# Order of the first loads, square buffers, and the places of u, the chunk inputs and po in a weight-streaming trunk

## The chip, the cores and the metric

The kernel runs on one core of one Trainium2 chip. The metric is the device time of one execution in microseconds. Three runs of the kernel before gave 935.23, 936.41 and 936.98 us, a median of 936.41 us.

The engines are TensorE (PE in the profile; PEld is its weight load), VectorE (DVE), ScalarE (ACT), GpSimd (POOL) and SyncE (SP). Here SyncE issues nearly all transfers.

## The reference

Two layers with D = 2048 and 256 positions. In each, one projection of the normalised input feeds two groups of heads: differential attention and a diagonal state space (S5).

```
for l in range(2):
    h = rmsnorm(x, pre_norm_g[l])
    q, k, v, z_att, u, z_ssm = split(h @ w_in[l])          # 6 x 1024 columns
    w = softmax(q1 k1 + bias) - lam * softmax(q2 k2 + bias)  # 8 heads, chunk-causal mask
    o_att = rmsnorm(w @ v) * (1 - lam_init) * silu(z_att)
    y = s5_ssm(u)             # 64 groups of 16 channels, 64 complex states each, scan over positions
    g_val, g_gate = split(gelu(y) @ w_glu[l])
    o_ssm = g_val * sigmoid(g_gate) * silu(z_ssm)
    x = x + rmsnorm(concat(o_att, o_ssm) @ w_out[l])
```

## The kernel before

**Streaming.** All weights of both layers lie in one tensor of 144 chunks, taken in 288 half-steps of 512 KB (`raw`, 128 x 1024 float32), 144 to a layer. `emit_dma` (line 197) issues the load of a half-step on SyncE's queue into one of five buffers, in order; a load waits on the queue until its buffer is free, and what is written behind it on that queue waits too. Each half-step is split for TensorE: ScalarE copies it to `hi` (rounded, line 158), VectorE subtracts to get `lo` (line 140). Then `main` issues the half-step's matmuls into a PSUM bank `ac` of a pool of four banks: weights hi with both pieces of h (`ht`), and lo with the first. In layer 0 the half-steps of u, q and k have 24 matmuls, in layer 1 (`JOIN`) 16, most others 12.

**Order in a layer.** Half-steps 0 to 7 give the first four blocks of u by another split of the work (four `ac` banks, all held until u is evacuated), 8 to 15 the remaining u chunks 4 to 7, 16 to 47 q and k, then v and the gates, the GLU and the output projection. The index of a half-step within its layer is `s`.

**What runs beside it.** Everything else is written as Python generators that are woven into the half-steps: each half-step advances every live generator to its next `yield` (ahead of its lo), and after its matmuls those that stand at `yield 1` or `yield 2`, up to a fixed allowance. So one further `yield` puts what follows it one half-step later in the order of every engine. Short VectorE operations that generators append to `urgent` or `weave` are filled in around the lo of a half-step.

- `rstd_gen` computes the pre-norm. In layer 0: squares of x on ScalarE and sums on VectorE (`sq`), `psv` on TensorE, Newton steps on VectorE, `psr` on TensorE, `rbc` on ScalarE. Only then can VectorE make `u` from the held banks, which also frees them. Two of the u chunks (4 and 5) accumulate in banks of the other PSUM pool (`acu`).
- `u_store` and `u_load` (lines 678 and 687) write u to DRAM and read it back in another layout (`U`), in two halves, called from `hooks` at fixed `s`.
- `s_gen` makes the chunk inputs: it copies into H behind the matmuls `pss` of U with `wi`, in four parts of two blocks; the scan follows on VectorE. The third and fourth part wait for `u2`, which says that the second half of U is there.
- `pv_gen`, one per head: transposes the attention weights, copies them to `wt` (ScalarE), multiplies with v (`po`), squares and gates; every fourth head starts the Newton steps of the head norm (`scal`).

**The start.** `load_x` and `load_w0` bring the first two 128-column slices of x (on ScalarE's queue) and the first weight in two halves (on SyncE's); `build0(k)` makes h's two pieces of slice k, of which half-step 0 needs the first for its first half and the second for its second. Half-step 1 needs the next weight. W0 is a number of warm-up matmuls ahead of it.

Of the kernel before, what the change touches and what calls it, by code (L numbers as in the profile page):

```python
# [14 lines left out]
ALU = mybir.AluOpType  # L15
# [10 lines left out]
MAGIC = 12582912.0  # L26
SC = 57
Y0 = (80, 77)
W0 = 18
PS = 4  # L30
TB = 38
PG = 1
# [10 lines left out]
LB = 2  # L43
SX = 144
NA = 2
JOIN = (1,)
TPS = ([(0, 1024), (1024, 1024)], [(0, 512), (512, 768), (1280, 768)])
WY = 2
# [36 lines left out]
def hybrid_trunk(ctx: ExitStack, tc, x, rel_bias, post_norm_g, xt_in, wst, vecs, poles, lams, bc, onehot, out):  # L85
# [16 lines left out]
    def R(i, name, dt=F32):  # L102
        return rp.tile([128, 2048], dt, tag=f"r{i}", name=name)

    def side(name):
        return pb.tile([128, 512], F32, tag="side", name=name)

    def acc(name):
        return pa.tile([128, 512], F32, tag="acc", name=name)
# [29 lines left out]
    def tt(o, a, b, op):  # L139
        V.tensor_tensor(o, a, b, op=op)  # L140
        return cost(o)
# [15 lines left out]
    def act(o, i, f, **kw):  # L157
        A.activation(out=o, in_=i, func=f, **kw)  # L158
# [153 lines left out]
    def until(key):  # L312
        while key not in S:
            yield
# [310 lines left out]
    def rstd_gen(l):  # L625
        if l == 0:

            X = S["xT"].rearrange("p k c -> p (k c)")
            sq = R(1, "sq")
            a, b = sq[:, 0:1024], sq[:, 1024:2048]  # L630
            act(a, X[:, 0:1024], AF.Square)
            yield
            for n in range(1, 4):
                act(b, X[:, 1024 * n:1024 * n + 1024], AF.Square)
                yield
                tt(a, a, b, ALU.add)
            for n in (512, 256):
                tt(a[:, 0:n], a[:, 0:n], a[:, n:2 * n], ALU.add)
            yield 1
            psv = side("psv")  # L640
            for t in range(2):
                mm4(psv[:, 2 * t:2 * t + 2], a[:, 128 * t:128 * t + 128], ones[:, 0:2], True, True)
        else:
            xt = S["xt"]
            for n in range(4):
                for t in range(2):
                    j = tmp5("junk")
                    act(j, xt[t][:, 512 * n:512 * n + 512], AF.Square, accum_out=ssx[:, t, n:n + 1])
                yield
        dg = tmp("dg")  # L650

        def ops():
            v = st.tile([128, 2], F32, tag="nv", name="nv")
            if l == 0:
                ts(v, psv[:, 0:4:2], EPS * D, None, ALU.add)
            else:
                V.tensor_reduce(out=v, in_=ssx, axis=AX.X, op=ALU.add)
            yield 70
            yield from newton_ops(rst[:, 0], v, 2)
            yield ts(rst[:, 1], rst[:, 0], -0.5 * NK * DK, None, ALU.mult)  # L660
            yield ts(rst[:, 0], rst[:, 0], -NK * DK, None, ALU.mult)
            for t in range(2):
                yield ts(dg[:, 128 * t:128 * t + 128], ident, rst[:, 0, t:t + 1], None, ALU.mult)
            S[f"rst{l}"] = True

        urgent.append(ops())
        yield from until(f"rst{l}")
        yield 1
        ps = side("psr")
        mm4(ps[:, 0:256], ones, dg, True, True)  # L670
        act(rbc, ps[:, 0:256], AF.Copy)
        S[f"rbc{l}"] = True
        yield


    def u_store(b0):
        cut = lambda t: t.rearrange("p (m b c) -> p m (b c)", m=4, b=8)[:, :, 64 * b0:64 * b0 + 256]
        SY.dma_start(out=cut(uds), in_=cut(S["u"]))
# [34 lines left out]

    def s_gen(l):
        yield from until(f"wa{l}")
        H = rp.tile([128, 2, NPAIR, 64], F32, tag="big", name="H")
        S["H"] = H
        G.memset(H[:, :, :, 0:1], 0.0)
        U = S["U"]
        for b0 in range(0, 8, 2):  # L720
            while b0 >= 4 and not (S["u2"] and f"wi{l}" in S):
                yield
            yield 2

            pss = [side("pss") for _ in range(2)]
            for b in (b0, b0 + 1):
                wi = S[f"wi{l}" if b >= 4 else f"wa{l}"][b // 4]
                for h in range(2):
                    for a in range(2):
                        for r, g in ((0, 0), (1, 1), (1, 0), (0, 1)):  # L730
                            rows, o = slice(64 * g, 64 * g + 64), 64 * (g ^ r)
                            q, c = 2 * h + r, 256 * a + 64 * (2 * (b - b0) + h)
                            mm4(pss[r][o:o + 64, c:c + 64], wi[rows, b % 4, 2 * q + a], U[rows, 8 * q + b], True, True)
            yield
            for r, ps in enumerate(pss):
                psv = ps.rearrange("p (a j c) -> p a j c", a=2, j=4)
                hv = H[:, :, 4 * b0 + r:4 * b0 + 8:2]
                act(hv[:, :, :, 16:64], psv[:, :, :, 0:48], AF.Copy)
                act(hv[:, :, :, 1:16], psv[:, :, :, 48:63], AF.Copy)
        weave.append(scan_ops(l))  # L740
        yield

        src = uds.rearrange("(q g n) (m r) -> g m n q r", q=4, g=2, m=4)
        dst = U.rearrange("p (q b) c -> p q (b c)", q=4)
        for d in range(2):
            for m in range(4):
                r = 64 * d + 16 * m
                SY.dma_start(out=dst[r:r + 16, 1::2], in_=src[1 - d, m, :, 1::2])
            yield
# [130 lines left out]
    def pv_gen(l, h):  # L880
        yield from until(f"w{l}{h}")
        v, za, s1 = S["v"], S["za"], S["as"]
        w_ = S["att"][:, 384 * (h % 4):384 * (h % 4) + 384]
        yield 1
        ps = side("pwt")
        for j in range(3):
            tpose(ps[:, 128 * j:128 * j + 128], w_[:, 128 * j:128 * j + 128], ident)
        yield
        wt = scp.tile([128, 384], F32, tag="wt", name="wt")
        act(wt, ps[:, 0:384], AF.Copy)  # L890
        yield 1
        po = side("po")
        vv = v.rearrange("p (t c) -> p t c", t=2)[:, :, 128 * h:128 * h + 128]
        mm4(po[:, 0:128], wt[:, 256:384], vv[:, 0], True, True)
        mm4(po[:, 128:256], wt[:, 0:128], vv[:, 0], True, False)
        mm4(po[:, 128:256], wt[:, 128:256], vv[:, 1], False, True)
        yield
        for b in range(2):
            j = tmp("junk")
            act(j[:, 0:128], po[:, 128 * b:128 * b + 128], AF.Square, accum_out=s1[:, 2, 2 * h + b:2 * h + b + 1])  # L900
        zv = za.rearrange("p (t c) -> p t c", t=2)[:, :, 128 * h:128 * h + 128]
        mul(zv, zv, po[:, 0:256].rearrange("p (t c) -> p t c", t=2))
        S[f"att{l}{h}"] = True
        if h % 4 == 3:
            w = slice(2 * (h - 3), 2 * (h - 3) + 8)
            sc = st.tile([128, 8], F32, tag=f"scal{h // 4}", name="scal")
            lam_init = 0.8 - 0.6 * math.exp(-0.3 * l)

            def ops():
                a = st.tile([128, 8], F32, tag="a8", name="a8")  # L910
                yield mul(a, s1[:, 2, w], s1[:, 0, w])
                yield stt(a, a, 1.0 / 128, s1[:, 0, w], ALU.mult, ALU.mult)
                yield ts(a, a, EPS, None, ALU.add)
                yield from newton_ops(sc, a, 8)
                yield stt(sc, sc, -NK * (1.0 - lam_init), s1[:, 0, w], ALU.mult, ALU.mult)
                yield mul(sc.rearrange("p (h t) -> p h t", t=2), sc.rearrange("p (h t) -> p h t", t=2),
                          rst[:, 1].unsqueeze(1).to_broadcast([128, 4, 2]))
                S[f"scal{l}{h // 4}"] = sc

            yield  # L920
            urgent.append(ops())
# [87 lines left out]
    def main(hs, only=None, part=None):  # L1009
# [29 lines left out]
            done = b == 3 and h == 1  # L1039
        elif seg in ("u", "q", "k"):  # L1040
            if h == 0:
                S["acc"] = [side("acu") if i % LAYER in (4, 5) else acc("ac")]
            o = S["acc"][0][:, 0:256]
            hv = hi.rearrange("p (k c) -> p k c", k=8)
            lv = lo.rearrange("p (k c) -> p k c", k=8)
# [72 lines left out]
    def hooks(l, s):  # L1118
# [27 lines left out]
                SY.dma_start(out=S["xt"][t], in_=src[128 * t:128 * t + 128])  # L1146
        if s == 11:
            S["U"] = rp.tile([128, NPAIR, 64], F32, tag="U", name="U")
        if s in (14, 19):
            u_store(0 if s == 14 else 4)  # L1150
        if s in (15, 20):
            u_load(0 if s == 15 else 4)
        if s == 15:
            at(cur[0], s_gen(l))
        if s == 21:
            at(cur[0], toep_gen(l))
        S["u2"] = s >= 22
        S["zfree"] = s >= 113
        S["wfree"] = l > 0
        for h in range(8):  # L1160
# [19 lines left out]
    with tc.manual_schedule():  # L1180
# [9 lines left out]
        def load_w0(p):  # L1190
            c = slice(512 * p, 512 * p + 512)
            SY.dma_start(out=raw[0][:, c], in_=wst[0][:, c])


        load_params()
        raw[0] = wp.tile([128, 1024], F32, tag="raw", name="raw")
        load_w0(0)
        load_x(A, 0, 1)
        load_x(A, 1, 2)
        load_w0(1)  # L1200
        act(cf[:, 0, 0:2], ones[:, 0:2], AF.Tanh)
        emit_dma(1)
# [162 lines left out]
```

## Time and profile before

| | |
|---|---|
| median of three runs | 936.41 us |
| profiled execution | 934.74 us |
| its span | 933.0 us |
| TensorE busy | 905.2 us (97%) |
| VectorE busy | 672.1 us (72%) |
| ScalarE busy | 486.4 us (52%) |
| mean granted clock of TensorE | 0.987 |
| mean rate of the transfers | 189 GB/s |

The span runs from the first to the last instruction that the profiler recorded; the time is a little longer. Busy times count instructions that work, not those that wait. The granted clock is a share of TensorE's full speed: 1.0 is 2.4 GHz, 0.5 is 1.2 GHz. In a timeline row the bracket gives the idle time of that engine ahead of the row and what ended it.

### The profile page before, as it was taken

To read this page: it belongs to the slowest core of one execution; us is meant where nothing else is said; L and a number is where in the kernel's file an instruction comes from. 1 tells how busy PE (TensorE), PEld (TensorE's weight loads), DVE (VectorE), ACT (ScalarE), POOL (GpSimd) and SP (SyncE) were. 2 spreads that over 40 slices of the span, in tenths; PEclk is the share of its full clock that TensorE was granted. 3 is DMA by queue.
4 is the path that set the end of the run, shared out by engine and by line. 5 is a ranking of instruction groups with operands and counts; after the bars stand their busy time and mean duration, and the time that the engine had idled before them with its cause. 6 is when DMAs were issued, how large, how long until landed. Compare 5 with 4: busy or idle time off the path is not lost.

```text
span 933.0 us, 16359 instructions
## 1 busy us (share of the span) xinstructions
PE 905.2 (97%) x6354; PEld 778.5 (83%) x6354; DVE 672.1 (72%) x1202; ACT 486.4 (52%) x878; POOL 13.7 (1%) x19
## 2 busy tenths in 40 slices
PE   8999999999999999999999899999999999999995
PEld 8889999878778788888889688888888788888884
DVE  5878995898974757898576448899876466665464
ACT  5533348375365776444469344445565565644451
POOL 2000000000000000000000000000000000000001
PEclk9999999999999999999999999999999999999998
DMA  8657574775453477576645655865545346665752
GB/s 310 198 172 252 183 213 141 186 236 164 153 181 114 118 244 230 177 248 226 213 161 182 213 173 144 262 195 173 172 141 176 112 156 189 197 211 171 289 185 91
DMA packets 65069, 176.11 MB, mean 189 GB/s; under 512 B 17574, under 2 KB 24512, under 8 KB 64096
## 3 DMA queue, kind: packets, MB, share of 16 engines
q1 hardware_dynamic: 64416, 174.63, 59.1%
q8 instruction: 50, 0.82, 0.4%
q10 hardware_dynamic: 432, 0.29, 0.1%
q14 instruction: 27, 0.22, 0.1%
q0 software_dynamic: 144, 0.15, 0.0%
HBM read 167.42 MB, written 7.88 MB: 188 GB/s over the span
## 4 chain that ended last, share of the span: by engine, by line
PE 87%; DVE 6%; ACT 2%; DMA 2%; issue 1%; SPq 0%; ACTq 0%; DVEq 0%
PE ac L137 77%; PE acu L137 3%; DVE lo L140 2%; PE lga L137 1%; PE po L137 1%; PE psy L137 1%; DMA xT<-in_xt_dram 1%; PE pss L137 1%; DVE H L140 1%; PE psw L121 1%; ACT hi L158 1%; DVE sct L140 1%; DMA uds<-u 1%; DVE sq L140 1%; ACT y L158 0%
## 5 line engine op out<-in xcount | busy, mean ns | idle before, releaser
L158 ACT ACTIVATE hi<-raw 128x1024 fp32r<-128x1024 f32 (+1 forms) x282 | 297.7, 1057 | 360.6 <-PE ac L137 303.4
L140 DVE TENSOR_TENSOR lo<-raw,hi 128x1024 fp32r<-128x1024 f32 (+1 forms) x282 | 342.7, 1218 | 128.1 <-ACT hi L158 126.5
L137 PE MATMUL ac<-ht,hi 128*128 128x256 f32 (+1 forms) x1120 | 259.5, 318 | 4.3 <-DVE u L140 2.1
L137 PE MATMUL ac<-hi,ht 128*128 128x512 f32 x768 | 249.3, 396 | 0.0
L137 PEld LDWEIGHTS ac<-ht,hi 128*128 128x128 f32 x1120 | 187.4, 194 | 19.1 <-ACT hi L158 4.5
L137 PE MATMUL ac<-ht,lo 128*128 128x256 f32 x704 | 200.7, 286 | 0.6 <-DVE lo L140 0.6
L137 PEld LDWEIGHTS ac<-hi,ht 128*128 128x128 f32 x768 | 144.2, 188 | 31.5
L137 PE MATMUL ac<-lo,ht 128*128 128x512 f32 x384 | 150.3, 391 | 1.5 <-DVE lo L140 1.4
L137 PE MATMUL ac<-hi,mx 128*128 128x512 f32 x456 | 141.9, 390 | 0.0
L137 PEld LDWEIGHTS ac<-ht,lo 128*128 128x128 f32 x704 | 136.3, 194 | 1.1 <-DVE lo L140 1.1
L137 PEld LDWEIGHTS ac<-hi,mx 128*128 128x128 f32 x456 | 85.6, 188 | 17.9
L137 PE MATMUL ac<-lo,mx 128*128 128x512 f32 x228 | 88.7, 389 | 0.0
L137 PEld LDWEIGHTS ac<-lo,ht 128*128 128x128 f32 x384 | 72.2, 188 | 17.5 <-DVE lo L140 3.7
L137 PE MATMUL ac<-hi,ghi 128*128 128x512 f32 x128 | 51.6, 403 | 0.0
L137 PE MATMUL ac<-hi,glo 128*128 128x512 f32 x128 | 50.2, 392 | 0.0
L137 PEld LDWEIGHTS ac<-lo,mx 128*128 128x128 f32 x228 | 42.8, 188 | 8.7
L137 PE MATMUL ac<-lo,ghi 128*128 128x512 f32 x128 | 49.9, 390 | 0.0
L158 ACT ACTIVATE att<-att,mx 128x128 f32<-128x128 f32 x64 | 28.4, 446 | 4.8 <-DVE mx L863 4.2
L147 DVE SCALAR_TENSOR_TENSOR y<-y 128x512 f32<-128x512 f32 x16 | 11.0, 690 | 26.9 <-ACT y L158 26.9
L137 PEld LDWEIGHTS ac<-hi,glo 128*128 128x128 f32 x128 | 24.0, 188 | 5.3
L137 PEld LDWEIGHTS ac<-lo,ghi 128*128 128x128 f32 x128 | 24.1, 188 | 4.5
L137 PEld LDWEIGHTS ac<-hi,ghi 128*128 128x128 f32 x128 | 24.1, 188 | 4.5
(202 smaller groups left out, 963.4 us busy)
## 6 DMA issues: line engine op xcount, KB each, us to landing
raw<-in_wst_dram SPq DMA_DIRECT2D x287, 512.0 KB, 3.8
U<-uds SPq DMA_DIRECT2D x48, 64.0 KB, 2.5
bt<-in_bc_dram SPq DMA_DIRECT2D x4, 512.0 KB, 6.2
uds<-u SPq DMA_DIRECT2D x4, 512.0 KB, 5.0
pg<-in_post_norm_g_dram SPq DMA_DIRECT2D x2, 1024.0 KB, 6.9
xt<-in_x_dram SPq DMA_DIRECT2D x2, 1024.0 KB, 7.2
xt<-xsave SPq DMA_DIRECT2D x2, 1024.0 KB, 6.4
tabs<-tab SPq DMA_DIRECT2D x1, 1536.0 KB, 9.1
```

The lines of the kernel that those rows point to most:

```text
L121: P.transpose(o, i, idn)
L137: P.matmul(o, lhsT=l, rhs=r, start=start, stop=stop, skip_group_check=True)
L140: V.tensor_tensor(o, a, b, op=op)
L147: V.scalar_tensor_tensor(out=o, in0=a, scalar=s, in1=b, op0=op0, op1=op1)
L158: A.activation(out=o, in_=i, func=f, **kw)
```

## The change

- The two first slices of x move from ScalarE's queue to SyncE's, in the order slice 0, half weight 0, slice 1, half weight 1. W0 goes from 18 to 13.
- The four squares get a buffer each, in two more tiles. One `yield` more stands ahead of `psv`, and in layer 0 one more ahead of `psr`.
- In layer 0 the u chunks 4, 5 and 6 accumulate in the other pool, in layer 1 only chunk 4 (before, 4 and 5 in both).
- `u_store` comes at s = 15 and 20 in layer 0 and at 11 and 18 in layer 1 (before, 14 and 19 in both), the loads one half-step behind it.
- `s_gen` starts one half-step later and has another `yield` ahead of its third part.
- In `pv_gen`, `wt` comes from a pool with two buffers (before, one), and `po` one half-step later.

Order on SyncE at the start, before: the row that is not a weight is the later slices of x, the first two slices being on ScalarE's queue.

```order
L1192 DMA raw<-in_wst_dram 128x512 x2
L197 DMA raw<-in_wst_dram 128x1024
L1188 DMA xT<-in_xt_dram 128x512
L197 DMA raw<-in_wst_dram 128x1024
L1188 DMA xT<-in_xt_dram 128x512
```

The same place after:

```order
L1197 DMA xT<-in_xt_dram 128x256
L1201 DMA raw<-in_wst_dram 128x512
L1197 DMA xT<-in_xt_dram 128x256
L1201 DMA raw<-in_wst_dram 128x512
L199 DMA raw<-in_wst_dram 128x1024
L1197 DMA xT<-in_xt_dram 128x512
```

The slices of 256 columns stand between the two halves of weight 0 and ahead of the next weight now.

Order on VectorE behind `psr` of layer 0, before; u is made from the acu banks, then from the four held banks ac0 to ac3, and the lo of the coming half-step follows:

```order
L140 TENSOR_TENSOR u_503<-acu_601,rbc_100 128x16x4x4
L140 TENSOR_TENSOR u_503<-acu_521,rbc_100 128x16x4x4
L140 TENSOR_TENSOR u_503<-ac0_175,rbc_100 128x16x4x4
L140 TENSOR_TENSOR u_503<-ac1_176,rbc_100 128x16x4x4
L140 TENSOR_TENSOR u_503<-ac2_177,rbc_100 128x16x4x4
L140 TENSOR_TENSOR u_503<-ac3_178,rbc_100 128x16x4x4
L140 TENSOR_TENSOR lo_674<-raw_501,hi_666 128x1024
```

After:

```order
L142 TENSOR_TENSOR u_495<-acu_671,rbc_100 128x16x4x4
L142 TENSOR_TENSOR u_495<-acu_594,rbc_100 128x16x4x4
L142 TENSOR_TENSOR u_495<-acu_504,rbc_100 128x16x4x4
L142 TENSOR_TENSOR u_495<-ac0_170,rbc_100 128x16x4x4
L142 TENSOR_TENSOR u_495<-ac1_171,rbc_100 128x16x4x4
L142 TENSOR_TENSOR u_495<-ac2_172,rbc_100 128x16x4x4
L142 TENSOR_TENSOR u_495<-ac3_173,rbc_100 128x16x4x4
L142 TENSOR_TENSOR lo_748<-raw_576,hi_739 128x1024
```

One product more stands ahead of ac0. On TensorE `psr` stands, after the change, two half-steps further on, between the last matmul into acu_671 and the first into ac_750, which takes the bank of ac0:

```order
L139 MATMUL acu_671<-ht_159,hi_622 128x256 x2
L139 MATMUL acu_671<-ht_159,lo_626 128x256
L139 MATMUL psr_734<-dg_532,ones_91 128x256
L139 MATMUL ac_750<-ht_159,hi_661 128x256 x2
L139 MATMUL ac_750<-ht_159,lo_663 128x256
```

Before, it stood in the same way between acu_601 and ac_676.

Order on SyncE around the store and loads of u in layer 1, before:

```order
L197 DMA raw<-in_wst_dram 128x1024 x11
L678 DMA uds<-u 512x1x256
L197 DMA raw<-in_wst_dram 128x1024
L687 DMA U<-uds 16x4x256 x8
L197 DMA raw<-in_wst_dram 128x1024 x4
L678 DMA uds<-u 512x1x256
L197 DMA raw<-in_wst_dram 128x1024
L687 DMA U<-uds 16x4x256 x8
```

After:

```order
L199 DMA raw<-in_wst_dram 128x1024 x8
L683 DMA uds<-u 512x1x256
L199 DMA raw<-in_wst_dram 128x1024
L692 DMA U<-uds 16x4x256 x8
L199 DMA raw<-in_wst_dram 128x1024 x6
L683 DMA uds<-u 512x1x256
L199 DMA raw<-in_wst_dram 128x1024
L692 DMA U<-uds 16x4x256 x8
```

The first store has moved ahead of three weight loads, the second ahead of one.

```diff
@@ -26,7 +26,7 @@
 MAGIC = 12582912.0
 SC = 57
 Y0 = (80, 77)
-W0 = 18
+W0 = 13
 PS = 4
 TB = 38
 PG = 1
@@ -43,6 +43,8 @@
 LB = 2
 SX = 144
 NA = 2
+ACU = ((4, 5, 6), (4,))
+US = ((15, 20), (11, 18))
 JOIN = (1,)
 TPS = ([(0, 1024), (1024, 1024)], [(0, 512), (512, 768), (1280, 768)])
 WY = 2
@@ -626,16 +628,17 @@
         if l == 0:
 
             X = S["xT"].rearrange("p k c -> p (k c)")
-            sq = R(1, "sq")
-            a, b = sq[:, 0:1024], sq[:, 1024:2048]
+            sq = [t[:, 1024 * i:1024 * i + 1024] for t in (R(1, "sq"), R(0, "sq")) for i in range(2)]
+            a = sq[0]
             act(a, X[:, 0:1024], AF.Square)
             yield
             for n in range(1, 4):
-                act(b, X[:, 1024 * n:1024 * n + 1024], AF.Square)
+                act(sq[n], X[:, 1024 * n:1024 * n + 1024], AF.Square)
                 yield
-                tt(a, a, b, ALU.add)
+                tt(a, a, sq[n], ALU.add)
             for n in (512, 256):
                 tt(a[:, 0:n], a[:, 0:n], a[:, n:2 * n], ALU.add)
+            yield
             yield 1
             psv = side("psv")
             for t in range(2):
@@ -665,6 +668,8 @@
 
         urgent.append(ops())
         yield from until(f"rst{l}")
+        if l == 0:
+            yield
         yield 1
         ps = side("psr")
         mm4(ps[:, 0:256], ones, dg, True, True)
@@ -713,12 +718,15 @@
 
     def s_gen(l):
         yield from until(f"wa{l}")
+        yield
         H = rp.tile([128, 2, NPAIR, 64], F32, tag="big", name="H")
         S["H"] = H
         G.memset(H[:, :, :, 0:1], 0.0)
         U = S["U"]
         for b0 in range(0, 8, 2):
-            while b0 >= 4 and not (S["u2"] and f"wi{l}" in S):
+            if b0 == 4:
+                while not (S["u2"] and f"wi{l}" in S):
+                    yield
                 yield
             yield 2
 
@@ -886,8 +894,9 @@
         for j in range(3):
             tpose(ps[:, 128 * j:128 * j + 128], w_[:, 128 * j:128 * j + 128], ident)
         yield
-        wt = scp.tile([128, 384], F32, tag="wt", name="wt")
+        wt = st.tile([128, 384], F32, tag="wt", name="wt")
         act(wt, ps[:, 0:384], AF.Copy)
+        yield
         yield 1
         po = side("po")
         vv = v.rearrange("p (t c) -> p t c", t=2)[:, :, 128 * h:128 * h + 128]
@@ -1039,7 +1048,7 @@
             done = b == 3 and h == 1
         elif seg in ("u", "q", "k"):
             if h == 0:
-                S["acc"] = [side("acu") if i % LAYER in (4, 5) else acc("ac")]
+                S["acc"] = [side("acu") if i % LAYER in ACU[l] else acc("ac")]
             o = S["acc"][0][:, 0:256]
             hv = hi.rearrange("p (k c) -> p k c", k=8)
             lv = lo.rearrange("p (k c) -> p k c", k=8)
@@ -1146,15 +1155,15 @@
                 SY.dma_start(out=S["xt"][t], in_=src[128 * t:128 * t + 128])
         if s == 11:
             S["U"] = rp.tile([128, NPAIR, 64], F32, tag="U", name="U")
-        if s in (14, 19):
-            u_store(0 if s == 14 else 4)
-        if s in (15, 20):
-            u_load(0 if s == 15 else 4)
+        if s in US[l]:
+            u_store(0 if s == US[l][0] else 4)
+        if s - 1 in US[l]:
+            u_load(0 if s - 1 == US[l][0] else 4)
         if s == 15:
             at(cur[0], s_gen(l))
         if s == 21:
             at(cur[0], toep_gen(l))
-        S["u2"] = s >= 22
+        S["u2"] = s >= US[l][1] + 3
         S["zfree"] = s >= 113
         S["wfree"] = l > 0
         for h in range(8):
@@ -1194,9 +1203,9 @@
 
         load_params()
         raw[0] = wp.tile([128, 1024], F32, tag="raw", name="raw")
+        load_x(SY, 0, 1)
         load_w0(0)
-        load_x(A, 0, 1)
-        load_x(A, 1, 2)
+        load_x(SY, 1, 2)
         load_w0(1)
         act(cf[:, 0, 0:2], ones[:, 0:2], AF.Tanh)
         emit_dma(1)
```

## Rows read from the trace of the kernel before

**Rows 1.** Page: busy time, share and instructions; a group: busy, mean ns, idle

```profile
PE 905.2 (97%) x6354; PEld 778.5 (83%) x6354; DVE 672.1 (72%) x1202; ACT 486.4 (52%) x878; POOL 13.7 (1%) x19
...
L147 DVE SCALAR_TENSOR_TENSOR y<-y 128x512 f32<-128x512 f32 x16 | 11.0, 690 | 26.9 <-ACT y L158 26.9
```

**Rows 2.** Waits of TensorE: us in total, times, longest

```profile
PE pss L137 <- DMA U<-uds: 4.4, 2, 2.8
PE ac L137 <- DVE u L140: 2.1, 1, 2.1
PE psv L137 <- DVE sq L140: 2.1, 1, 2.1
PE ac L137 <- DVE lo L140: 1.9, 5, 0.6
...
PE psx L121 <- DVE xt L147: 1.5, 1, 1.5
PE po L137 <- ACT wt L158: 1.4, 2, 1.0
...
PE pss L137 <- ACT H L158: 1.0, 2, 0.7
```

**Rows 3.** Stretches: us, busy of PE, PEld, DVE, ACT, POOL, granted clock, DMA share, GB/s

```profile
1.70:7.00 5.30, 5.30 (x38) 5.30 (x38) 0.93 (x2) 2.51 (x4) 3.84 (x5) 1.00 0.96 284
10.90:14.31 3.41, 3.41 (x16) 3.41 (x17) 3.27 (x5) 3.41 (x7) 0.00 (x0) 0.50 1.04 413
38.21:41.62 3.41, 3.41 (x17) 3.41 (x17) 3.25 (x17) 0.00 (x0) 0.00 (x0) 0.50 0.41 147
533.14:536.55 3.41, 3.41 (x60) 3.00 (x50) 0.00 (x0) 1.20 (x4) 0.00 (x0) 0.50 0.58 232
```

**Rows 4.** Chain that ended last: start us, us, what

```profile
10.84 8.72 PE ac L137 x58
38.47 13.06 PE acu L137 x96
...
96.40 31.87 PE ac L137 x264
...
522.22 4.84 DMA uds<-u
...
539.50 14.33 PE ac L137 x80
```

**Rows 5.** Timeline of several engines up to 38 us: start us, us, what

```profile
1.65 0.43 SPq L197 DMA_DIRECT2D raw<-in_wst_dram  x1
...
9.04 0.51 ACT L158 ACTIVATE ht<-xT,prm 128x256 fp32r<-128x256 f32 x1 [2.52 <-DMA xT<-in_xt_dram]
9.45 1.56 ACT L158 ACTIVATE hi<-raw 128x512 fp32r<-128x512 f32 x2
...
11.04 1.22 DVE L140 TENSOR_TENSOR lo<-raw,hi 128x1024 fp32r<-128x1024 f32 x1 [0.26 <-ACT hi L158]
12.19 0.87 DVE L147 SCALAR_TENSOR_TENSOR ht<-xT,prm,ht 128x256 fp32r<-128x256 f32 x2
...
10.12 0.51 PE L137 MATMUL ac<-ht,hi 128*128 128x256 f32 x2 [1.85 <-ACT hi L158]
...
13.11 0.63 PE L137 MATMUL ac<-ht,hi 128*128 128x256 f32 x2
...
37.80 0.67 PE L137 MATMUL psv<-ones,sq 128*128 128x2 f32 x4 [2.08 <-DVE sq L140]
```

**Rows 6.** Transfers issued from 0.7 to 2.1 us: KB each, us to landing

```profile
raw<-in_wst_dram SPq DMA_DIRECT2D x1, 512.0 KB, 7.2
```

**Rows 7.** Timeline of VectorE at the squares and the u products

```profile
35.34 2.41 DVE L140 TENSOR_TENSOR sq<-sq 128x1024 f32<-128x1024 f32 x3
...
53.33 1.99 DVE L140 TENSOR_TENSOR u<-ac,rbc 128x256 f32<-128x256 f32 x4
...
505.47 2.06 DVE L140 TENSOR_TENSOR u<-ac,rbc 128x256 f32<-128x256 f32 x4 [0.88 <-ACT rbc L158]
```

## The prediction, made before the changed kernel was run

> **What bounds the kernel now.** I read the page's busy times first: TensorE works through 905.2 of 933.0 us [rows 1], so the kernel ends when TensorE has done its list, and an edit on another engine is worth something only where TensorE waits for that engine. The second view is therefore the table of TensorE's waits [rows 2]: few, and nearly all in a handful of places. The third is the granted clock by stretches. After some waits TensorE runs at 0.50, the 1.2 GHz level, for 3.41 us, busy throughout [rows 3]; such a wait costs twice, once idle and once in slow matmuls. The timeline and the chain then place each wait. A matmul of the kind that fills the list takes 31.87/264 = 0.1207 us at full clock [rows 4], and a half-step has 24 of them (2.9 us), in layer 1 for u, q and k 16.
>
> The sum is made against the profiled execution (span 933.0, 934.74 in all). The three timed runs have their median at 936.41, 1.67 above it; I add that at the end.
>
> **Start.** Before, the second slice of x was issued by ScalarE and landed at 9.04, where ScalarE had waited 2.52 us for it [rows 5]. The second half of half-step 0 waited for it, and half-step 1, whose hi is the second copy in the row at 9.45, had its first matmul at 13.11. Now slice 0, half weight 0, slice 1, half weight 1 and weight 1 stand on one queue. Half-step 0 can then run early (with 5 warm-up matmuls fewer ahead of it), and half-step 1 is bounded by its own weight. That was issued at 1.65 [rows 5] and took 7.2 us [rows 6], so it landed at 8.85. After landing come hi (1.56 for a half copy and a whole one, so about 1.04), lo 1.22 and half of the 0.87 for the pieces of h, with gaps 2.75 [rows 5]. Lower bound of the landing: the queues moved 284 GB/s from 1.7 to 7 us [rows 3], 1.5 MB, and about as much must be in by then (two weights of 512 KB, two slices of 128 KB, tables of some 170 KB): 6.9. Upper bound: it now stands fifth on the queue instead of third, two issues of 0.43 later [rows 5], and with the same 7.2 lands at 9.7. I take 8.2, near the middle: the engines were 0.96 busy in that stretch [rows 3], so bytes count more than the issue, and fewer of them stand ahead. Half-step 1 then begins at 8.2 + 2.75 = 10.95, 2.16 earlier. Against that, the slow stretch: the 58 matmuls from 10.84 took 8.72 us where full clock needs 58 x 0.1207 = 7.0 [rows 4], a part of it under half-step 0's rest; now all of it falls on half-step 1 behind a longer wait, for which I take off 0.75. Gain **1.4**, bounds -0.3 and 3.
>
> The Trainium skill, "DMA: Bandwidth & Descriptors", section "Issuing engines are not separate DMA queues", says that transfers started by different engines run on the same 16 DMA engines and interleave, and that a second issuing engine saves sequencer time only. By it one queue brings order but no bandwidth; if the order did nothing for weight 1, it would land at 8.85 again and the gain would be 0.8 instead of 1.4. The row of 284 GB/s has several engines issuing and no row has SP alone at this place, so nothing here decides it.
>
> **Squares.** With two buffers each further square on ScalarE waited for VectorE's sum; the last sums ended at 35.34 + 2.41 = 37.75 [rows 7], and TensorE waited 2.08 us for them [rows 2, 5]. Four buffers take ScalarE out of the alternation, and psv comes one half-step later. TensorE was free at 37.80 - 2.08 = 35.72 [rows 5]; with 2.9 us of matmuls more it reaches psv at 38.6, behind even the old finish. So the wait goes. Behind it the 96 matmuls took 13.06 us against 96 x 0.1207 = 11.59 [rows 4]; the clock drop there [rows 3] goes with the wait, 1.47. Gain 2.08 + 1.47 = **3.55**, bounds 2 and 3.6.
>
> **u and its banks.** Behind psr VectorE makes the u products, four in 1.99 us from the first four banks [rows 7], after two from the acu banks, and the next half-step waits for the first of those banks: 2.1 us [rows 2]. In the order psr still stands directly ahead of the half-step that needs a bank, and three acu products instead of two stand ahead of the first ac product. So this wait stays and grows by one product, 1.99/4: **-0.5**, bounds -0.6 and the first rival. Its slow stretch stays and adds nothing.
>
> **pss, scan, po.** pss waited 1.0 us in two pieces for ScalarE's H copies [rows 2]; it comes one half-step later, and 2.9 us cover that: **+1.0**. Five waits for lo make 1.9 us, the longest 0.6 [rows 2]; those under layer 0's scan are some two thirds. The scan starts two half-steps later and ends one interval later, so part of its work leaves the crowded steps, while the rest meets other work: **+0.7**, bounds -1 and 1.9. Each po group comes a half-step behind its copy wt, which has two buffers; that covers 1.4 us [rows 2]: **+1.3**, with 0.1 off for the crowd at layer 0's end, bounds -1.2 and 1.4. If this cover is gone, what is late next is y: VectorE already waits 26.9 us for ScalarE's y, off TensorE's path so far [rows 1].
>
> **u in layer 1.** The biggest term. pss waited twice for the load of U, 4.4 us in all [rows 2]; the load follows a store that left at 522.22 and took 4.84 [rows 4]. The data were ready long before: the first u products ended at 505.47 + 2.06 = 507.5 [rows 7]. What held the store is its place on SP, behind weight loads that wait for a free buffer; the order now has 8 of them ahead where 11 were. Three half-steps of 14.33/80 x 16 = 2.87 [rows 4] are 8.6 us. So U is there 8.6 us earlier, and pss comes one half-step later: the 4.4 us are covered with 8.6 + 2.87 - 4.4 = 7 to spare. The weight loads behind the U loads are held as long as before, three half-steps earlier. The low stretch behind the wait [rows 3] goes too: 3.41 us of busy TensorE at half the rate are 1.7 lost. Gain 4.4 + 1.7 = **6.1**, bounds 3 (if pss's second part still waits) and 6.1.
>
> psx's wait for xt, 1.5 [rows 2], is touched by no edit.
>
> **The sum.** 1.4 + 3.55 - 0.5 + 1.0 + 0.7 + 1.3 + 6.1 = 13.55. 934.74 - 13.55 = 921.2; with 1.67 for the timed runs, 922.9 us.
>
> **Rivals.** *The u wait goes as well* (8%): Newton gets longer, so TensorE may find its bank. Worth 2.1 + 0.5 and a slow stretch of 1.5 as behind psv, 4.1 more: 918.8. Against it: however early Newton ends, rbc and four products come after psr, which TensorE runs just before it needs the bank. *The crowd moves to layer 0's end* (14%): the scalar Newton behind po now meets y and the gate one half-step later. For one interval there I count lo 1.22 [rows 5], y 0.69 a piece [rows 1], that Newton and small products, an estimate of 3.7 us in a half-step of 2.9: two such cost 1.6, and with a slow stretch of 1.5 some 3.1 goes: 926. For it speaks y's wait, against it that no wait for y reaches TensorE in rows 2. *Slower: the clock does not come back after the start* (5%). The wait between half-steps 0 and 1 grows from 1.85 [rows 5] to some 3.3, and TensorE stays at 1.2 GHz until the place of psv. Its work from 14.31, where the low stretch ended [rows 3], to 35.72 would take 21.4 us longer: 936.41 + 21.4 - 13.55 = 944; it decides from 13.6 us of such work. Against it: each low stretch in rows 3 ended by itself, also that behind the longest wait, 2.8. *The store leaves no earlier* (5%): if SP is held by something else than its place, 6.1 is lost: 929.
>
> **How the numbers follow.** The forecast as summed has 68%. A difference under 0.2% (1.9 us) could not be told from no change. All cases but the slow clock end further below 936.41 than that, 95%; of these I set 3 aside for several small mishaps that add up to no change: faster 0.92, same 0.03, slower 0.05. The range goes from 917 (start and scan at their better bounds, or the first rival with one of them) to 929 (the crowd with a start that brings nothing, or the store held); outside lie the slow clock and a pile of good or bad ends.
>
> **What would show it.** Right: no wait of TensorE over 0.5 us for U, sq, wt or H; the first U load of layer 1 landed several us before pss; half-step 1's first matmul near 11; the wait for u still there, about 2.5; 0.50 at the start, at u and at psx, none at psv and none ahead of layer 1's scan. Wrong: a new wait over 1 us at layer 0's end, hi copies late for weights behind the earlier store in layer 1, or 0.50 through the 20s of us.

## The result, and the profile after

The changed kernel takes 924.26 us in the median of four runs (921.94 to 925.00), the kernel before 936.02 in the runs beside it: a ratio of 0.987, interval 0.985 to 0.989. The forecast was 922.9. The gain is 11.8 us between these medians, where 13.55 had been summed. The profiled execution took 924.31 us with a span of 922.5, which is 10.5 shorter than the span before.

First the page of the changed kernel, busy time by engine, and then its table of TensorE's waits:

```profile
PE 901.3 (98%) x6344; PEld 775.3 (84%) x6344; DVE 674.2 (73%) x1202; ACT 487.1 (53%) x878; POOL 13.7 (1%) x19
```

```profile
PE ac L139 <- DVE u L142: 2.5, 1, 2.5
PE ac L139 <- DVE lo L142: 2.4, 4, 0.9
PE psg L123 <- DVE nwh L142: 2.2, 1, 2.2
PE psx L123 <- DVE xt L149: 1.5, 1, 1.5
...
PE ac L139 <- DVE ht L149: 0.9, 1, 0.9
PE pss L139 <- ACT wi L160: 0.3, 1, 0.3
```

Against [rows 2] the waits for U, sq, wt and H are gone, that for u has grown from 2.1 to 2.5, that for lo from 1.9 to 2.4, and one is new: psg, 2.2. TensorE's busy time fell by 3.9 us. Ten warm-up matmuls fewer have no part in it (the warm-ups kept TensorE busy for 6.8 us before and 7.0 after, more of them at the slow clock), so these are slow matmuls that became fast. The stretches at 0.50 between the first speed-up and the last matmuls are three now, where the trace of before had five ([rows 3] shows three of them):

```profile
55.00:58.41 3.41, 3.41 (x19) 3.41 (x18) 1.27 (x3) 0.23 (x1) 0.00 (x0) 0.50 0.24 52
314.41:317.82 3.41, 3.08 (x7) 2.48 (x8) 2.84 (x5) 3.03 (x6) 0.00 (x0) 0.50 0.48 153
471.43:474.84 3.41, 3.35 (x15) 3.35 (x16) 3.19 (x7) 2.91 (x7) 0.00 (x0) 0.50 0.33 117
```

To price each term I took matmuls that stand at one place of the program in both profiles, and subtracted their starts. The lead of the changed kernel grows or shrinks from one to the next by what lies between; these are two single executions:

| matmul | before, us | after, us | lead | term | gained | predicted |
|---|---|---|---|---|---|---|
| psp, behind half-step 2 | 19.49 | 17.27 | 2.22 | start | 2.2 | 1.4 |
| first of half-step 10 | 45.62 | 39.22 | 6.40 | squares | 4.2 | 3.55 |
| pst of layer 0 | 128.20 | 122.19 | 6.01 | u and its banks | -0.4 | -0.5 |
| lga, first | 183.34 | 176.57 | 6.77 | pss | 0.8 | 1.0 |
| lga, 17th | 259.59 | 252.65 | 6.94 | scan | 0.2 | 0.7 |
| psg, second | 310.22 | 302.99 | 7.23 | po, layer 0 | 0.3 | 1.3 with layer 1 |
| psg, fourth | 324.57 | 321.55 | 3.02 | layer 0's end | -4.2 | 0 (a rival: -3.1) |
| psu of layer 1 | 553.67 | 544.33 | 9.34 | u in layer 1 | 6.3 | 6.1 |
| psg, last | 771.61 | 761.12 | 10.49 | po, layer 1 | 1.2 | as above |

(For psg a number counts groups of four matmuls.) The biggest single loss is at layer 0's end. VectorE's timeline there, and GpSimd's one row in the same stretch:

```profile
307.93 0.17 DVE L149 SCALAR_TENSOR_TENSOR nwh<-nwh 128x8 f32<-128x8 f32 x1
308.02 1.85 DVE L154 TENSOR_SCALAR a<-a 128x8 f32<-128x8 f32 x1
308.14 1.74 DVE L149 SCALAR_TENSOR_TENSOR nwy<-nwh,nwy 128x8 f32<-128x8 f32 x1
309.93 0.17 DVE L142 TENSOR_TENSOR nwh<-nwy 128x8 f32<-128x8 f32 x1
```

```profile
308.04 1.81 POOL L475 MEMSET cm<- 128x2048 f32 x1 [143.38 <-PE psz L139]
```

An operation on eight numbers a partition takes 1.85 us where its like takes 0.17, and it ends when GpSimd's fill of cm ends (308.04 + 1.81 = 309.85). TensorE pays for it at psg and at the lo behind it, and the clock drops:

```profile
313.01 0.63 PE L123 MATMUL psg<-ident,y 128*128 128x128 f32 x4 [2.15 <-DVE nwh L142]
...
314.74 0.79 PE L139 MATMUL ac<-lo,ht 128*128 128x512 f32 x1 [0.86 <-DVE lo L142]
```

The releaser named, nwh, is the last operation of VectorE before; what psg reads is y.

### The profile page after: what moved, and what is told of

It reads as the page before. It is cut to its first block, busy times and chain, and to the rows that moved or that the text cites. A ratio compares the mean times of both kernels' runs of the same rounds, so it can differ in the third digit from the quotient of the medians.

```text
span 922.5 us, 16345 instructions
## 1 busy us (share of the span) xinstructions
PE 901.3 (98%) x6344; PEld 775.3 (84%) x6344; DVE 674.2 (73%) x1202; ACT 487.1 (53%) x878; POOL 13.7 (1%) x19
## 4 chain that ended last, share of the span: by engine, by line
PE 86%; DVE 4%; ACT 2%; issue 1%; DVEq 0%; ACTq 0%
PE ac L139 78%; PE lga L139 1%; DVE lo L142 1%; PE psy L139 1%; PE po L139 1%; ACT wi L160 1%; PE pss L139 1%; DVE sct L142 1%; PE acu L139 1%; ACT hi L160 1%; PE pwt L123 1%; PE pst L139 0%; PE psm L123 0%; PE psf L123 0%; DVE nwh L142 0%
## 5 line engine op out<-in xcount | busy, mean ns | idle before, releaser
L139 PEld LDWEIGHTS ac<-ht,hi 128*128 128x128 f32 x1104 | 184.3, 193 | 18.9 <-issue 2.9
```

Source lines behind the costliest of these rows:

```text
L139: P.matmul(o, lhsT=l, rhs=r, start=start, stop=stop, skip_group_check=True)
```

## The experiments

Medians of kernels that ran side by side can be compared with each other; the kernel before, run beside them, scattered by 7 to 8 us, so the small terms are read from the traces.

**The changed kernel again.** No edit.

> The changed kernel once more. In its first profile TensorE waited 2.15 us for psg and 0.86 for lo near 313 us (layer 0's end) and a low-clock stretch followed; in that place one VectorE operation of 128x8 took 1.85 us where its like takes 0.17. Theory: the crowd on VectorE there (y, glo, zs and the head norm's Newton steps in one interval) belongs to the change and returns in every execution: wait of 0.4 to 2.2 us for psg and 0.9 for lo, 924 us. Rival: the slow operation is an accident of that one execution; without it the waits are under 1.3 us together, no low stretch follows, and the time is near 921.9, the lowest of the four runs shown.

Measured: 922.78 us (920.67 to 925.48), and the same slow operation, beside the same fill:

```profile
307.97 1.85 DVE L154 TENSOR_SCALAR a<-a 128x8 f32<-128x8 f32 x1
```

```profile
307.99 1.81 POOL L475 MEMSET cm<- 128x2048 f32 x1 [143.00 <-PE psz L139]
```

It was no accident of one execution: the profiles of two kernels below that keep both the fill and the later po (psr earlier, s_gen as before) show the same 1.85 and 1.86 us. The rival falls.

**Zeros of cm from ScalarE.**

```diff
-        G.memset(cm, 0.0)
+        if l:
+            act(cm, ones[:, 0:1].to_broadcast([128, 2048]), AF.Copy, scale=0.0)
+        else:
+            G.memset(cm, 0.0)
```

> The changed kernel with one fill moved: the zeros of cm for layer 1 come from ScalarE and not from GpSimd. In the two profiles of the changed kernel the slow VectorE operation (a<-a, 128x8, 1.85 us) begins within 0.1 us of GpSimd's fill of cm (1.81 us) and ends with it. Theory (VectorE's operation waits for GpSimd's fill, 1.77 us, which the later po brought under the fill): the operation takes 0.17, the wait of psg falls from 2.15 to 0.4 or less, that of lo behind it stays or goes, and the low-clock stretch there goes if both are small: 923.5 less 1.8 to 4.2, 919.3 to 921.7. Rival (VectorE is simply overfull there): psg still waits over 1.5 us and the time stays within 1 us.

Measured: 920.93 us (919.58 to 922.96), 14.0 below the kernel before beside it; the changed kernel's two medians lay 11.8 and 10.3 below theirs. VectorE's same operation, and then TensorE's waits for psg and lo:

```profile
307.90 0.16 DVE L154 TENSOR_SCALAR a<-a 128x8 f32<-128x8 f32 x1
```

```profile
PE ac L139 <- DVE lo L142: 2.6, 5, 0.9
...
PE psg L123 <- DVE nwh L142: 0.6, 1, 0.6
```

psg's wait fell by 1.6, and no low stretch followed there. From the second to the fourth group of psg TensorE took 15.57 us, where the changed kernel took 18.56 and the kernel before 14.35: 3.0 of the 4.2 were the fill's. So VectorE's operation had waited for GpSimd's fill. 0.6 and the 0.9 for lo remain; they are the crowd itself. The Trainium skill, "SBUF — State Buffer", section "Who interferes with whom", says that `tensor_scalar` on VectorE can use the pair of ports that it shares with GpSimd, and that one of the two then stands still until the other has finished. The three profiles agree: 1.85 beside the fill, 0.16 without it. Another fill, of t, shows the same away from TensorE's path. In the kernel with s_gen as before it began 0.34 us ahead of a copy on VectorE, which took 1.51 us where the profile of the kernel before has 0.22:

```profile
78.09 1.51 DVE L445 COPY a4s<-apow 128x64 f32<-128x64 f32 x1
```

```profile
77.75 1.81 POOL L698 MEMSET t<- 128x2048 f32 x1 [72.22 <-DMA uds<-u]
```

In the second of the combinations below VectorE came 0.08 us first; its operation took 0.19 and the fill 1.86:

```profile
77.48 0.19 DVE L154 TENSOR_SCALAR a<-a 128x64 f32<-128x64 f32 x1
```

```profile
77.56 1.86 POOL L699 MEMSET t<- 128x2048 f32 x1 [72.02 <-DVE a L149]
```

At the fill of cm VectorE's record begins 0.02 us ahead, and yet it was VectorE that waited; why, these records don't show. In the kernel before the fill ran from 315.27 to 317.08, over operations on two tensors, and none of them was slow.

**po as before.** In pv_gen:

```diff
-        wt = st.tile([128, 384], F32, tag="wt", name="wt")
+        wt = scp.tile([128, 384], F32, tag="wt", name="wt")
         act(wt, ps[:, 0:384], AF.Copy)
-        yield
         yield 1
```

> The changed kernel with pv_gen as before the change (one wt buffer, po without the further half-step). Theory (the later po pushes the head norm's Newton steps into y's interval): the waits for psg and lo near 313 us and their low stretch go, 4.2 us back; the waits for wt return, 1.45 us: 924.3 - 2.8 = 921.5. Rival (the crowd there has nothing to do with po): psg's wait stays and 1.45 us are added: 925.7.

Measured: 921.65 us (920.95 to 921.99), against 922.78 of the changed kernel beside it, whose runs (920.67 to 925.48) overlap with these. Its waits:

```profile
PE ac L139 <- DVE lo L142: 2.2, 5, 0.6
...
PE po L139 <- ACT wt L160: 1.4, 2, 1.0
```

psg is not in the list any more, and no low stretch lies there; wt is back with 1.4. So it was the later po that brought the operation under the fill. The whole edit on po gained 1.45 us and cost 4.2 in the profiles: a loss of some 2.7.

**psr one half-step earlier.**

```diff
         yield from until(f"rst{l}")
-        if l == 0:
-            yield
         yield 1
```

> The changed kernel with psr one half-step earlier (the further yield ahead of it taken out), so that a whole half-step into an acu bank stands between psr and the matmul that needs the first held bank. Theory (the wait for u comes from psr standing directly ahead of that matmul): the wait of 2.5 us goes, with its low stretch of 1.5 to 1.7: 924.3 - 4.1 = 920.2. Rival (VectorE's Newton steps are late, so that psr itself waits): psr waits for dg instead by up to 2.9 us and the time stays within 1 us of 924.3.

Measured: 919.56 us (918.38 to 921.60), 3.2 below the changed kernel beside it. Its longest waits:

```profile
PE ac L139 <- DVE lo L142: 2.2, 5, 0.6
PE psg L123 <- DVE nwh L142: 2.2, 1, 2.2
PE psx L123 <- DVE xt L149: 1.5, 1, 1.5
```

The wait for u is gone, and psr does not wait instead, so the rival falls. With psr next to the matmul that needs the bank, rbc and four products lie open; with one half-step between, they are covered.

**Squares, and u in the other pool.** The kernel before with these edits of the change, the second `yield` ahead of psr left out:

```diff
-            sq = R(1, "sq")
-            a, b = sq[:, 0:1024], sq[:, 1024:2048]
+            sq = [t[:, 1024 * i:1024 * i + 1024] for t in (R(1, "sq"), R(0, "sq")) for i in range(2)]
...
+            yield
             yield 1
             psv = side("psv")
...
-                S["acc"] = [side("acu") if i % LAYER in (4, 5) else acc("ac")]
+                S["acc"] = [side("acu") if i % LAYER in ACU[l] else acc("ac")]   # ((4, 5, 6), (4, 5))
```

> The kernel before with four square buffers, psv one half-step later and chunks 4 to 6 of u in the other pool in layer 0, but without the further half-step ahead of psr. Theory: the wait of psv (2.08) and that for u (2.08) both go, with a low stretch each (1.5): 7 us less than the kernel before. Rival (VectorE's Newton steps become late): psr or the u wait takes back 1 to 3 us of it.

Measured: 926.29 us beside 934.94, ratio 0.990 (0.987 to 0.994). Neither psv nor u is in its list of waits; from psp to pst it took 100.68 us where the kernel before took 108.71, so 8.0 us are won there. But U has grown:

```profile
PE pss L138 <- DMA U<-uds: 5.8, 2, 4.3
```

Its lead over the kernel before fell from 9.7 us in the half-steps ahead of pss to 7.4 behind it. So 2.3 us of what is gained early are given back at U in layer 1, with a store of 6.21 us, where [rows 4] has 4.84, and a stretch at 0.50 of 6.83 instead of 3.41.

**u of layer 1 alone.**

```diff
+US = ((14, 19), (11, 18))
...
-        if s in (14, 19):
-            u_store(0 if s == 14 else 4)
+        if s in US[l]:
+            u_store(0 if s == US[l][0] else 4)
...
-        S["u2"] = s >= 22
+        S["u2"] = s >= US[l][1] + 3
```

> The kernel before with only the places of the store and loads of u changed, and these only in layer 1 (11 and 18 instead of 14 and 19). pss itself stays where it was. Theory (place on SP's queue): U lands 8.6 us earlier, both waits of pss (2.83 and 1.58) and the low stretch behind them go: 936.2 - 6.2 = 930.0. Rival (the gain needs pss one half-step later too): 1 to 2 us of wait stay with the low stretch, 932 to 934.

Measured: 925.78 us (923.22 to 929.32) beside 933.12, ratio 0.9925 (0.990 to 0.995): 7.3 us. TensorE does not wait for U at all in its trace, with pss at its old place; the rival falls. Its lead over the kernel before grows from 2.95 us in the half-steps ahead of pss to 9.20 behind its second part: 6.25, as expected. (The last line of the edit also lets the last two parts of pss start one half-step earlier.)

**The start alone.** W0 = 13 and:

```diff
-        load_w0(0)
-        load_x(A, 0, 1)
-        load_x(A, 1, 2)
+        load_x(SY, 0, 1)
+        load_w0(0)
+        load_x(SY, 1, 2)
         load_w0(1)
```

> The kernel before with the start alone: the two slices of x on SyncE's queue in order of use, 13 warm-up matmuls. The prediction's 1.4 us for it: psp, which follows half-step 3, at 18.1 instead of 19.5. The changed kernel's four profiles had it at 17.2 to 17.9, the kernel before at 19.5 and, with the same start, once at 18.1. Theory (order of landing): psp at 17.2 to 17.9, no low stretch before 37 us, the time 0.3 to 2.3 below the kernel before. Rival (the later slices and squares had a part in it): psp at 18 or later.

Measured: 933.87 us (928.53 to 936.54) beside 934.94, ratio 0.998 (0.996 to 1.0005): not told from no change, nor from the forecast 1.4. psp stood at 17.65, 1.84 earlier than in [rows 5]'s profile, and no low stretch before 36. The profiled execution was the slowest of its ten, 936.54 us, and its trace shows where the 1.84 went, first the wait at U and then the chain's row of the store:

```profile
530.94 0.30 PE L137 MATMUL pss<-U,wi 64*64 64x64 f32 x2 [4.49 <-DMA U<-uds]
```

```profile
520.62 6.30 DMA uds<-u
```

The store left 1.6 us earlier and took 6.30 where it had taken 4.84 [rows 4]; pss began at 530.94, before at 530.88. That does not happen always: with four warm-ups, the next experiment, the lead ahead of pss was 3.8 and 2.85 of it remained behind.

**Four warm-up matmuls instead of 13**, the loads as in the start alone.

> The kernel before with the start's loads on SyncE's queue and 4 warm-up matmuls instead of 18 (13 in the change). In the changed kernel the warm-ups end at 5.3 to 6.6 us, and half-step 0's first half is ready by 5.3. Theory (weight 1's landing bounds half-step 1): psp stays at 17.2 to 17.9, the waits ahead of half-step 0 and 1 grow by 1 to 2 us without cost. Rival (the warm-ups are what brings TensorE's clock up early, and idle time brings it down): 0.50 reaches into half-step 1 or 2, psp 0.8 to 1.8 later, above 18.2.

Measured in one execution: 934.04 us, psp at 18.58, against 17.65 with 13. TensorE's first matmuls ran at the slow pace, after a wait of 1.50 behind the warm-ups, and the full clock was granted at 14.23 only:

```profile
9.36 0.63 PE L137 MATMUL ac<-ht,hi 128*128 128x256 f32 x2
```

In the changed kernel, with 13, such a pair took 0.40 at 9.41, the full clock being granted at 7.21. The warm-ups thus brought the full clock earlier, though nothing reads them; the rival's psp above 18.2 came true. In this one execution they would have saved 0.9 us at psp against the start alone, 0.7 to 1.4 against all ten profiles with 13.

**s_gen as before**, in the changed kernel:

```diff
         yield from until(f"wa{l}")
-        yield
...
-            if b0 == 4:
-                while not (S["u2"] and f"wi{l}" in S):
-                    yield
+            while b0 >= 4 and not (S["u2"] and f"wi{l}" in S):
                 yield
```

> The changed kernel with s_gen as before (no further yields). Theory of the prediction: pss waits 1.0 us again for H, and the five waits for lo under layer 0's scan, 1.26 us in the changed kernel, come back to 1.35 (0.1 more, and not 0.7 as predicted). Rival (the prediction's 0.7): 1.9 or more for lo there.

Measured in one execution: 923.68 us. H is back with 1.0, as expected; against both expectations no wait over 0.1 us for lo is left under the scan. What remains is two waits, at layer 0's end and a small one:

```profile
PE ac L139 <- DVE lo L142: 1.1, 2, 0.9
```

So, beside the other edits, the edit to s_gen gained 0.7 to 0.8 at pss and cost 1.3 in waits under the scan, and it is other edits that would have emptied the scan's stretch.

**Combinations.** psr earlier and cm on ScalarE:

> The changed kernel with psr one half-step earlier and the fill of cm on ScalarE. If the two losses are separate they add: 919.6 (psr earlier alone) less 1.8 to 4.2: 915.4 to 917.8. If the clock only loses its low stretches elsewhere instead, 918 to 919.6.

Measured: 917.54 us (915.59 to 919.03), ratio to before 0.981 (0.979 to 0.984). Then also po later in layer 1 only (`if l: yield`):

> The kernel with psr one half-step earlier and the fill of cm on ScalarE, and po later by a half-step in layer 1 alone. Theory (the later po of layer 0 still crowds VectorE: 0.57 for psg and 0.87 for lo): these 1.4 us go, the wait for wt of layer 0 (0.47) returns: 0.9 us less, 916.6. Rival (crowding has nothing to do with po): no gain, 917.5 to 918.

Measured: 916.46 us (915.32 to 916.99), ratio 0.981 (0.978 to 0.984); psg is not among its waits, wt has 0.5. That wait is at the po of layer 0, 0.47 where the kernel before has 0.46, although wt has its two buffers there: what covers it in the changed kernel is the later po, not the second buffer. And with the old s_gen on top:

> psr one half-step earlier, the fill of cm on ScalarE, po later in layer 1 alone, and s_gen as before the change. Theory (the profile of the changed kernel with the old s_gen showed no wait over 0.1 us for lo under layer 0's scan, and pss 0.96 for H): against the same kernel with the later s_gen, 1.6 us of waits for lo go, 0.96 for H instead of 0.23 return: 0.9 less, 915.6. Rival (the scan's waits depend on where psr and po stand too): the waits for lo stay over 1 us and the time is 916.5 to 917.2.

Measured: 916.57 us (916.37 to 917.04), ratio 0.983 (0.980 to 0.985). Its five waits for lo make 1.9 us again, and H 1.0: the rival was right, the scan's waits depend on where psr and po stand too. The last two are not told from each other.

## Why the prediction was right, and where it was not

**Right.** The time was 1.4 us above the forecast, and its two biggest terms have the mechanism and the size named. U in layer 1 was held by the store's place on SyncE's queue: that edit alone took every wait for U away and gained 6.25 in its profile, and the changed kernel gained 6.3, where 6.1 was forecast. In the changed kernel the store left 11.5 us earlier than in [rows 4], 8.5 of it beyond the lead of 3.0 that this kernel has there (8.6 were forecast), and the first pss came at 527.76:

```profile
510.69 0.56 SPq L683 DMA_DIRECT2D uds<-u  x1
516.78 3.66 SPq L692 DMA_DIRECT2D U<-uds  x8
```

What the move saves differs between executions: in the four profiles with the store at its old place TensorE waited 4.4, 5.8, 6.0 and 6.2 us for U, with a store of 4.84, 6.21, 6.30 and 5.88. [rows 4] has the shortest of them, which fits the 7.3 of the timed runs. The squares brought 4.2 for 3.55: the wait, the slow stretch, 0.2 in psv's own matmuls and 0.5 in half-steps 6 and 7. The later psv did that, as the forecast's sum says, and hardly the four buffers. The sums ended at 35.05, and TensorE began half-step 8 at 33.02, so that psv at its old place would still have waited some 2 us (an estimate from these two rows; no run has the buffers alone):

```profile
32.65 2.40 DVE L142 TENSOR_TENSOR sq<-sq 128x1024 f32<-128x1024 f32 x3
```

```profile
33.02 0.40 PE L139 MATMUL acu<-ht,hi 128*128 128x256 f32 x2
```

The wait for u stayed and grew by 0.4 for 0.5, and the experiment with psr earlier shows the reason given: psr directly ahead of the matmul that needs the bank. The waits for wt brought 1.45 for 1.3, pss 0.8 for 1.0.

**Near by luck in part.** Term by term the profiles differ from the sum by +0.8 at the start, +0.6 at the squares, +0.2 at U and +0.1 each at u and at po's waits, against -4.2 at layer 0's end, -0.5 at the scan and -0.2 at pss. The forecast came as close as 1.4 us also because these partly cancel, and because the kernel before stood 0.4 lower in the runs beside the changed kernel. One of the forecast's own signs of being wrong appeared: a new wait over 1 us at layer 0's end.

**The start, right in size by offsetting errors.** 2.2 between the profiles for 1.4; but the old start scatters. In three profiles with it psp stood at 19.49, 19.32 and 18.09, the first two with a stretch at 0.50 from 11 us on and the third without; in the ten with the new start and 13 warm-ups at 17.45 in the mean (17.19 to 17.91), none with such a stretch. The means, 18.97 and 17.45, differ by 1.5. The parts are not those of the forecast. Weight 1 landed later than the 8.2 that I took: its hi copy began at 8.69 after a wait for it. The 2.75 from there hold, 8.69 + 2.75 = 11.44, but for half-step 1's second matmul, which needs the piece of h that VectorE makes; the first does not and began at 10.20, not 10.95:

```profile
8.69 1.06 ACT L160 ACTIVATE hi<-raw 128x1024 fp32r<-128x1024 f32 x1 [0.63 <-DMA raw<-in_wst_dram]
```

```profile
11.45 0.38 PE L139 MATMUL ac<-ht,hi 128*128 128x256 f32 x1 [0.87 <-DVE ht L149]
```

And no low stretch came, so the 0.75 taken off was not lost. The rival of a clock that does not come back had the sign wrong for this edit: TensorE came out of the warm-ups busy, and its longest wait up to psp was 0.87. With four warm-ups a slow first half-step did come, and the clock came back at 14.23, not at the place of psv; the 21 us of that rival are seen nowhere.

**The scan, a step that failed.** I reasoned that part of the scan "leaves the crowded steps", 0.7. It was 0.2, and with the old s_gen there were no waits over 0.1 us there at all, so later pieces do not leave the crowd by themselves. The experiments say that the waits hang on which pieces stand between two lo copies, with psr and po among them; that the order alone would have given the size was not tried.

**Layer 0's end, a rival that came true beside the forecast.** "The crowd moves to layer 0's end" was given 14% and 3.1 us; 4.2 came. In the sum the term for po had "0.1 off for the crowd at layer 0's end" and a lower bound of -1.2; with the 4.2 the edit on po made some -2.7. The crowd was as named, y beside the head norm's Newton steps, but most of the price was not in my count of VectorE's work: 3.0 of the 4.2 went with GpSimd's fill, some 1.6 us of VectorE waiting and the slow stretch that followed. The prediction names no work of GpSimd at that place. I had compared the order of each engine with its own order before, and not what runs at the same time on two engines.

## What to carry to other kernels

When an edit moves small VectorE operations by a step, look at which GpSimd instruction runs at that time; a fill of 1.8 us can hold up a VectorE operation of 0.17. A store that others wait for belongs as far up an in-order queue as its data allow, and its gain should be sized with the range that the transfer takes from execution to execution. Give a matmul that produces something a whole step before the matmul that needs what comes of it, and read gains by the lead of a fixed matmul between two profiles: part of an early gain can go at the next wait for a transfer (1.0, 2.3 and 2.5 us here in three profiles where U was late), and one profile is not enough for a term of a microsecond or two.

## What was not expected of the hardware

The same wait is not always followed by a slow clock. psx waited 1.5 us in all 14 profiles; a stretch at 0.50 began within 2.1 us of its end in seven of them, the two of the changed kernel and that of the kernel before among them, and not in the other seven, as psr earlier, cm on ScalarE or u of layer 1 alone. After the wait for U it lasted 3.41 us in one profile and 6.83 in three. With 1.5 to 1.7 us a stretch, this makes executions of one kernel differ; whether it accounts for all of their scatter was not settled. The start also moves by itself: psp stood at 19.49, 19.32 and 18.09 in three profiles whose start was that of the kernel before, and a stretch at 0.50 began at 11 us in the first two alone.
